# Seven block products from tile 8 of phase 0, their results in a stream of their own, and the RWKV jobs' state chain in two PSUM banks

## The chip, the cores and the metric

The kernel runs on one core of a Trainium2 chip. The metric is device time in microseconds (us) for one execution. Three runs of the kernel before gave 2259.75, 2262.86 and 2265.27 us; the median is 2262.86 us. A difference of about 0.2% (4.5 us) is what a measurement of this kernel can tell from none.

## The reference

One decoder layer is applied to a prompt of 1024 tokens and to eight single-token samples. Everything is float32; the model width is 1024 and the hidden width of the FFN 2816.

```python
h = x + 0.5 * rmsnorm(swiglu(rmsnorm(x, n1), gate1, up1, down1), n1_post)
proj = rmsnorm(h, n_mix) @ w_in                # 3328 columns
ya = differential attention (4 heads)          # of the first 1536 columns
yb = rwkv7_time_mix (8 heads of 64)            # of the other 1792
h = h + rmsnorm(concat(ya, yb) @ w_out, n_mix_post)
h = h + 0.5 * rmsnorm(swiglu(rmsnorm(h, n2), gate2, up2, down2), n2_post)

# rwkv7: per head and token, a state s (64 x 64)
sa = s @ (-kk_t)
s  = s * w_t + outer(sa, kk_t * a_t) + outer(v_t, k_t);   y_t = s @ r_t
```

It returns the layer's output, the keys and values, and the last states.

## The kernel before, in words

**Phases and halves.** The tokens are cut in two halves of 512 (one of them with the eight sample columns, 520). The first FFN is phase 0 (half 0) and phase 1 (half 1), the second FFN phase 2 and phase 3. Between them each half goes through the projection (stream `proj`), the RWKV part (streams `job0`, `job1`), attention (`attn0`, `attn1`), the output projection (`out` for half 0, `outb` for half 1). The FFN of one half fills TensorE while the mixing of the other half runs: phase 1 lies beside the mixing of half 0, phase 2 beside that of half 1. Phases 0 and 3 have no such neighbour.

**FFN.** `s_trunk` (L1034) goes over the 22 tiles of 128 hidden columns. A product in float32 accuracy is three matmuls in fp32r, with weights and data split into a high and a low part (`mm3`, L698). A plain tile takes gate and up for two column chunks of 256 or 264: 4 x 24 matmuls. In phases 0 and 3, from the tile that `FAST` names (L35), two tiles at a time are made with Strassen-like products instead (`seven`, L1098): the two tiles and the two column halves form a 2 x 2 block problem, and gate and up take 7 x 12 matmuls of 260 columns each in place of 8 x 12. `s_combine` (L994) makes the sums of the data blocks first and signals `combined`; `sums` (L940) makes the sums of the weight blocks. After each product VectorE adds it out of PSUM to the buffers v, and when a block is whole, `gates` (tanh and product) or `ups` (product, split into two parts) is applied to it; `late` and `was` hold these calls back by one product. `down` (L1160) then multiplies a finished group of tiles with the down weights and adds each result to the y tile (`trunk_xl0` in the profile's and the order's names) on VectorE. It runs behind the gate and up of the next group. The groups are in `GROUPS` (L102): for `FAST` 10, phase 0 has [0,1,2], [3,4], [5,6,7], [8,9] and then pairs; for `FAST` 8, [0,1,2], [3,4], [5], [6,7] and then pairs.

**Jobs.** `job` (L1680) is one pair of heads over 512 tokens in chunks of 64; four jobs in each half, two sets of buffers (job 0 and 2 are label `job0`, job 1 and 3 are `job1`). The front (mixing, norms; bank `dec`, and `cb` beside it) runs under the lock `front`, one job at a time. Then a job takes its set's lock and the bank `aux0` or `aux1`, builds the products of a chunk's rows (masked, `L`), transposes U (`pa`), multiplies `L` with R (`pv`, bank `cb`), solves a triangular system on VectorE (31 steps, by way of DRAM), and forms Z, L and R per chunk. Last comes the chain over the eight chunks: one PSUM tile takes Z times the state `Sd` and two products of L and R that don't need the state; VectorE makes the next `Sd` from it (`scalar_tensor_tensor`, L1915), ScalarE copies the outputs. In the names of the profile the state product is `job_aux<-bset_Sd,mix_X` (or `mix_T` in half 1), the state-free ones are `job_aux<-mix_X,job_w 128x64`.

**What sets the order.** Nothing runs as written. Each generator is a stream with a queue for each engine; every operation is recorded through one helper (so the profile shows L325 for all) and a list scheduler (`run`, L484) picks the next operation by an estimate of when it could start and how late it may be. Within one stream an engine's operations keep the order in which they were recorded; between streams only data, PSUM slots and locks count. A PSUM bank is handed from tile to tile in the order of recording. A stream may record up to 80 operations ahead (`AHEAD`, L91). The plan is made eight times and the best one by its own estimate is built, so a change in one place moves rows everywhere.

## Time and profile before

| | |
|---|---|
| median of three runs | 2262.86 us |
| the profiled execution | 2261.48 us, its span 2259.7 us |
| TensorE (PE) | 2197.5 us busy, 97% |
| VectorE (DVE) | 1556.7 us, 69% |
| ScalarE (ACT) | 1072.1 us, 47% |
| GpSimd (POOL) | 990.4 us, 44% |

In a row of the timeline the first number is the start and the second the length, both in us; `x12` is a count of merged instructions; the bracket gives the idle time of the engine just before it and who ended that. In a row of a stretch stand, behind its length, the busy times of PE, of its weight load, DVE, ACT and POOL, then the granted TensorE clock, the share of the DMA engines and GB/s. One fp32 matmul shows as two instructions, a transpose or an fp32r matmul as one. "Busy" of a PE row is modelled, with the pipeline's latency in it.

### The profile page before, as it was taken

To read this page: it belongs to the slowest core of one execution; us is meant where nothing else is said; L and a number is where in the kernel's file an instruction comes from. 1 tells how busy PE (TensorE), PEld (TensorE's weight loads), DVE (VectorE), ACT (ScalarE), POOL (GpSimd) and SP (SyncE) were. 2 spreads that over 40 slices of the span, in tenths; PEclk is the share of its full clock that TensorE was granted. 3 is DMA by queue.
4 is the path that set the end of the run, shared out by engine and by line. 5 is a ranking of instruction groups with operands and counts; after the bars stand their busy time and mean duration, and the time that the engine had idled before them with its cause. 6 is when DMAs were issued, how large, how long until landed. Compare 5 with 4: busy or idle time off the path is not lost. (4 is left out here: it accounts for less than half of the span.)

```text
span 2259.7 us, 42127 instructions
## 1 busy us (share of the span) xinstructions
PE 2197.5 (97%) x15575; PEld 1963.4 (87%) x15575; DVE 1556.7 (69%) x3577; ACT 1072.1 (47%) x2214; POOL 990.4 (44%) x818
## 2 busy tenths in 40 slices
PE   8999999999999999999999999999999999999998
PEld 8999998898877678987877777778888989999998
DVE  7757888656677667559585666786774366777776
ACT  6524444544453257444353445435664555444444
POOL 3525555533332573455353432345443355444443
PEclk9999999999999999999999999999999999999999
DMA  7322233445333574655464444486436848333433
GB/s 257 113 94 90 89 103 125 143 145 141 95 106 105 165 231 138 223 174 158 129 205 150 134 116 144 117 238 181 122 112 191 286 126 285 130 132 107 146 140 113
DMA packets 216998, 338.83 MB, mean 150 GB/s; under 512 B 50746, under 2 KB 131930, under 8 KB 216794
## 3 DMA queue, kind: packets, MB, share of 16 engines
q1 hardware_dynamic: 216506, 335.63, 47.5%
q8 instruction: 123, 2.02, 0.4%
q14 instruction: 81, 0.66, 0.1%
q10 hardware_dynamic: 288, 0.52, 0.1%
HBM read 281.06 MB, written 55.03 MB: 149 GB/s over the span
## 5 line engine op out<-in xcount | busy, mean ns | idle before, releaser
L325 POOL TENSOR_TENSOR wts_w<-wts_raw,wts_w 128x1024 fp32r<-128x1024 f32 (+2 forms) x156 | 295.5, 1901 | 363.9 <-ACT wts_w L325 314.0
L325 PE MATMUL trunk_m<-pre_X,wts_w 128*128 128x512 f32 (+3 forms) x2352 | 428.7, 336 | 9.5 <-ACT wts_w L325 6.7
L325 PE MATMUL trunk_m<-trunk_xl,wts_w 128*128 128x256 f32 (+2 forms) x2550 | 424.1, 318 | 7.9 <-DVE trunk_xl L325 5.3
L325 PEld LDWEIGHTS trunk_m<-pre_X,wts_w 128*128 128x128 f32 x2352 | 351.6, 191 | 51.3 <-ACT wts_w L325 5.6
L325 PEld LDWEIGHTS trunk_m<-trunk_xl,wts_w 128*128 128x128 f32 x2550 | 358.7, 189 | 40.1 <-DVE trunk_xl L325 7.0
L325 PE MATMUL trunk_m<-pre_T,wts_w 128*128 128x512 f32 (+3 forms) x2016 | 386.0, 343 | 3.3 <-DMA wts_w<-Lg 1.3
L325 PEld LDWEIGHTS trunk_m<-pre_T,wts_w 128*128 128x128 f32 x2016 | 307.6, 188 | 45.5 <-issue 4.8
L325 ACT CAST wts_w<-wts_raw 128x1024 fp32r<-128x1024 f32 (+3 forms) x299 | 244.5, 833 | 193.3 <-PE trunk_m L325 133.0
L325 PE MATMUL proj_m<-tail_xl,lin_w 128*128 128x256 f32 (+2 forms) x1920 | 322.4, 323 | 1.1 <-DVE init_E L325 0.7
L325 PEld LDWEIGHTS proj_m<-tail_xl,lin_w 128*128 128x128 f32 x1920 | 271.6, 189 | 36.1 <-issue 9.8
L325 DVE TENSOR_TENSOR trunk_xl<-trunk_xl,trunk_m 128x264 f32<-128x264 f32 (+2 forms) x343 | 165.1, 493 | 55.3 <-PE trunk_m L325 53.6
L325 POOL TENSOR_TENSOR lin_w<-lin_raw,lin_w 128x1024 fp32r<-128x1024 f32 x42 | 101.4, 2414 | 204.9 <-ACT lin_w L325 191.1
L325 POOL TENSOR_TENSOR trunk_xl<-trunk_t,trunk_xl 128x512 fp32r<-128x512 f32 (+3 forms) x81 | 88.4, 1092 | 179.4 <-ACT trunk_xl L325 179.1
L325 DVE TENSOR_TENSOR wts_w<-wts_raw,wts_w 128x1024 fp32r<-128x1024 f32 (+3 forms) x113 | 114.5, 1018 | 20.6 <-ACT wts_w L325 19.2
L325 ACT CAST lin_w<-lin_raw 128x1024 fp32r<-128x1024 f32 x52 | 54.5, 1049 | 94.1 <-PE proj_m L325 74.2
L325 ACT CAST wts_w<-wts_lraw 128x512 fp32r<-128x512 f32 x94 | 55.7, 619 | 67.4 <-DMA wts_lraw<-in_ffn_down_dram 28.3
L325 PE MATMUL trunk_aux<-trunk_xl,wts_w 128*128 128x264 f32 (+1 forms) x570 | 78.7, 284 | 0.0
L325 POOL TENSOR_TENSOR wts_w<-wts_lraw,wts_w 128x512 fp32r<-128x512 f32 x41 | 57.3, 1399 | 41.7 <-ACT wts_w L325 38.5
L325 PEld LDWEIGHTS trunk_aux<-trunk_xl,wts_w 128*128 128x128 f32 x570 | 72.6, 189 | 0.3 <-DVE trunk_hres L325 0.2
L325 ACT CAST wts_w<-wts_dec 128x512 fp32r<-128x512 f32 x30 | 17.6, 587 | 108.4 <-DVE wts_dec L325 108.4
L325 ACT CAST trunk_xl<-trunk_t 128x512 fp32r<-128x512 f32 (+3 forms) x96 | 46.3, 483 | 47.1 <-DVE trunk_t L325 45.3
L325 DVE TENSOR_TENSOR trunk_t<-trunk_g,trunk_m 128x512 f32<-128x512 f32 (+2 forms) x71 | 40.8, 576 | 35.9 <-PE trunk_m L325 30.7
(614 smaller groups left out, 4080.4 us busy)
## 6 DMA issues: line engine op xcount, KB each, us to landing
wts_raw<-in_ffn_gate_dram SPq DMA_DIRECT2D x87, 512.0 KB, 4.1
wts_raw<-in_ffn_up_dram SPq DMA_DIRECT2D x58, 512.0 KB, 3.6
lin_raw<-in_w_in_dram SPq DMA_DIRECT2D x52, 512.0 KB, 3.8
wts_raw<-in_ffn_down_dram SPq DMA_DIRECT2D x56, 384.0 KB, 3.4
wts_raw<-in_ffn_down_dram SPq DMA_DIRECT2D x29, 512.0 KB, 6.0
wts_w<-Ld SPq DMA_DIRECT2D x22, 512.0 KB, 3.8
mix_T<-out_dram SPq DMA_DIRECT2D x36, 256.0 KB, 3.1
Ld<-wts_w SPq DMA_DIRECT2D x24, 384.0 KB, 4.8
```

Of the source, the lines that this page charges most:

```text
L325: o = Op(eng, lambda: fn(*a, **k), st)
```

## The change

1. `FAST` of phase 0 goes from 10 to 8: tiles 8 and 9 are a pair for `seven` too, `combined` is due two tiles earlier, and the groups in front are those for 8. There is one group more, and tile 5 is a group by itself.
2. The calls of `gates` and `ups` in `seven` (phases 0 and 3) are recorded in a stream `use` of their own, not in the trunk's. On VectorE and ScalarE they need no longer come before what the trunk records after them.
3. In a job the transposes of U are 8 full 128 x 128 transposes in two groups of four with four copies, in place of 16 products of 64 x 64 with the identity and one copy.
4. The chain's tiles alternate between two banks, `aux0` and `cb` for `job0`, `aux1` and `dec` for `job1`. The state-free products come first in a tile, the state's product last.

```diff
-FAST = {0: 10, 3: 4}
+FAST = {0: 8, 3: 4}
...
-    def s_aside(self):
-        yield ("wait", "weights")
+    def s_aside(self, until="weights"):
+        yield ("wait", until)
...
+                def beside(fn, *a):
+                    was = self.cur
+                    self.cur = self.asides["trunk"]
+                    fn(*a)
+                    self.cur = was
...
                         for fn, *a in was:
-                            fn(*a)
+                            beside(fn, *a)
                         yield "pe"
                     for fn, *a in late:
-                        fn(*a)
+                        beside(fn, *a)
...
-        pa, pv = self.ps2().rearrange("p (n t) -> p n t", t=C), self.ps(bank="cb").rearrange("p (n t) -> p n t", t=C)
-        for n in range(NC):
+        pv = self.ps(bank="cb").rearrange("p (n t) -> p n t", t=C)
+        for g in range(2):
+            pa = self.ps2().rearrange("p (n w t) -> p n w t", n=4, w=2)
+            for n in range(4):
+                tr(two(pa[:, n]), two(U[:, 4 * g + n]), self.ident)
             for h, q in H:
-                mm(pa[q, n, :], U[q, n, h, :], self.ident[q, q], start=True, stop=True)
+                self.copy(U[q, 4 * g:4 * g + 4, 0, :], pa[q, :, h])
...
-        A.copy(U[:, :, 0, :], pa)
         A.copy(U[:, :, 1, :], pv)
...
         for n in range(NC):
-            pb = self.ps2().rearrange("p (n t) -> p n t", t=C)
-            mm(two(pb[:, 0:2]), two(Z[:, n]), two(Sd), start=True, stop=False)
+            pb = self.ps(bank=(f"aux{jb}", ("cb", "dec")[jb])[n % 2]).rearrange("p (n t) -> p n t", t=C)
             for h, q in H:
-                mm(pb[:, h], two(L[:, n, 2 * h:2 * h + 2]), R[:, n, h, :], start=False, stop=h == 1)
+                mm(pb[:, h], two(L[:, n, 2 * h:2 * h + 2]), R[:, n, h, :], start=h == 0, stop=False)
+            mm(two(pb[:, 0:2]), two(Z[:, n]), two(Sd), start=False, stop=True)
...
+    K.spawn(K.s_aside("trunk"), "use", (0, 3))
+    K.asides["trunk"] = K.streams[-1]
```

**First place, VectorE, the end of a pair in phase 0.** Before, the results of the second pair made by seven products (`trunk_g`, `trunk_t` with the buffers `init_rb`, `bset_sg`, `bset_la`) stand ahead of the down sums (`trunk_xl0`):

```order
L325 TENSOR_TENSOR bset_sg_30_133<-bset_la_29_132,trunk_aux0_343_2827 128x260
L325 TENSOR_TENSOR bset_la_29_132<-bset_la_29_132,trunk_aux1_344_2845 128x260
L325 TENSOR_TENSOR init_rb_10_113<-init_rb_10_113,trunk_aux1_344_2845 128x260
L325 TENSOR_TENSOR trunk_t_315_2612<-trunk_t_315_2612,bset_sg_30_133 128x260
L325 TENSOR_TENSOR init_rb_10_113<-init_rb_10_113,trunk_m0_346_2867 128x260
L325 TENSOR_TENSOR trunk_t_315_2612<-trunk_t_315_2612,bset_la_29_132 128x260
L325 TENSOR_TENSOR trunk_g_314_2611<-trunk_g_314_2611,init_rb_10_113 128x260
L325 TENSOR_TENSOR trunk_xl0_126_792<-trunk_xl0_126_792,trunk_m1_350_2894 128x256
```

Now the first down sum stands right behind the last product's sum, and the results come among the last of the sixteen down sums and behind them:

```order
L325 TENSOR_TENSOR trunk_xl0_126_796<-trunk_xl0_126_796,trunk_m0_338_2634 128x264
L325 SCALAR_TENSOR_TENSOR trunk_t_289_2245<-trunk_sq_304_2358,trunk_t_289_2245 128x260
L325 TENSOR_TENSOR trunk_xl0_126_796<-trunk_xl0_126_796,trunk_m1_339_2642 128x256
L325 TENSOR_TENSOR trunk_g_288_2244<-trunk_hres_231_1836,init_rb_10_113 128x260
L325 TENSOR_TENSOR trunk_xl0_126_796<-trunk_xl0_126_796,trunk_m2_340_2651 128x264
L325 SCALAR_TENSOR_TENSOR trunk_g_288_2244<-trunk_sq_307_2371,trunk_g_288_2244 128x260
L325 TENSOR_TENSOR trunk_g_288_2244<-trunk_g_288_2244,init_rb_10_113 128x260
L325 TENSOR_TENSOR trunk_t_289_2245<-trunk_t_289_2245,bset_sg_30_133 128x260
```

Before, three rows of results (`trunk_t` twice, `trunk_g`) stood between the sums and the first down sum; now they stand behind it, and in part behind all sixteen.

**Second place, TensorE, the chain of job 3 in half 0.** Before, a state product (`bset_Sd1`) and its state-free ones (`job1_w3`) stand together, all in the bank `aux1`, with six FFN matmuls between one step and the next:

```order
L325 MATMUL job1_aux1_1018_8905<-bset_Sd1_35_138,mix_X1_692_5440 128x128
L325 MATMUL job1_aux1_1018_8905<-mix_X1_692_5440,job1_w3_915_7821 128x64 x2
L325 MATMUL trunk_m1_1011_8820<-pre_T1_80_353,wts_w0_1005_8744 128x512
L325 MATMUL trunk_m1_1011_8820<-pre_T0_79_352,wts_w0_1005_8744 128x512 x2
L325 MATMUL trunk_m1_1011_8820<-pre_T1_80_353,wts_w0_1005_8744 128x512
L325 MATMUL trunk_m1_1011_8820<-pre_T0_79_352,wts_w0_1005_8744 128x512 x2
L325 MATMUL job1_aux1_1019_8917<-bset_Sd1_35_138,mix_X1_692_5440 128x128
L325 MATMUL job1_aux1_1019_8917<-mix_X1_692_5440,job1_w3_915_7821 128x64 x2
```

Now the banks `aux1` and `dec` take turns, the state-free products of a step stand ahead of its state product, behind the state product of the step before, and three to five FFN matmuls lie between:

```order
L325 MATMUL job1_aux1_1063_9097<-mix_X1_722_5502,job1_w3_945_7852 128x64 x2
L325 MATMUL job1_aux1_1063_9097<-bset_Sd1_35_138,mix_X1_722_5502 128x128
L325 MATMUL job1_dec_1064_9104<-mix_X1_722_5502,job1_w3_945_7852 128x64 x2
L325 MATMUL trunk_m1_1061_9064<-trunk_xl1_980_8105,wts_w1_1050_8946 128x512 x3
L325 MATMUL job1_dec_1064_9104<-bset_Sd1_35_138,mix_X1_722_5502 128x128
L325 MATMUL job1_aux1_1066_9124<-mix_X1_722_5502,job1_w3_945_7852 128x64 x2
L325 MATMUL trunk_m0_1062_9082<-trunk_xl1_980_8105,wts_w1_1050_8946 128x512 x5
L325 MATMUL job1_aux1_1066_9124<-bset_Sd1_35_138,mix_X1_722_5502 128x128
```

The steps stand closer, and the two kinds of product have changed places.

**Third place, TensorE, the chain of job 1 in half 0.** Before, its first two steps stand close together, among the transposes (`init_ident`) of job 2 and just behind the first row of job 3's front (`job1_dec` from `bset_wa`):

```order
L325 MATMUL job1_dec_872_7323<-bset_la_29_132,bset_wa_25_128 128x512
L325 MATMUL job1_aux1_891_7541<-job1_w3_778_6293,mix_X1_692_5440 64x128 x8
L325 MATMUL job0_aux0_858_7179<-init_ident_1_69,mix_X0_691_5439 64x64 x13
L325 MATMUL job1_aux1_893_7591<-bset_Sd1_35_138,mix_X1_692_5440 128x128
L325 MATMUL job1_aux1_893_7591<-mix_X1_692_5440,job1_w3_778_6293 128x64 x2
L325 MATMUL job0_aux0_858_7179<-init_ident_1_69,mix_X0_691_5439 64x64 x3
L325 MATMUL job0_cb_859_7180<-mix_X0_691_5439,job0_w2_851_7106 64x64 x8
L325 MATMUL job1_aux1_894_7598<-bset_Sd1_35_138,mix_X1_692_5440 128x128
```

Now the first step stands in the same surroundings, but the second is in `dec`, and stands behind the last product of job 3's front (`init_bones`), which has that bank:

```order
L325 MATMUL job1_dec_912_7413<-mix_T3_720_5500,init_bones_4_78 128x512
L325 MATMUL trunk_m1_956_7943<-trunk_dreg_680_5021,wts_w1_951_7925 128x512 x2
L325 MATMUL trunk_m0_957_7944<-trunk_dreg_680_5021,wts_w1_951_7925 128x512 x5
L325 MATMUL job1_dec_926_7654<-mix_X1_722_5502,job1_w3_809_6354 128x64 x2
L325 MATMUL job1_dec_926_7654<-bset_Sd1_35_138,mix_X1_722_5502 128x128
L325 MATMUL job1_aux1_928_7683<-mix_X1_722_5502,job1_w3_809_6354 128x64 x2
L325 MATMUL trunk_m0_957_7944<-trunk_dreg_680_5021,wts_w1_951_7925 128x512 x4
L325 MATMUL job1_aux1_928_7683<-bset_Sd1_35_138,mix_X1_722_5502 128x128
```

Eighty-four rows of TensorE's order lie between the first step's state product and the second's, where three lay between them before. In half 1 job 1's chain is parted in the same way.

More of the change, by code (lines that the diff above doesn't have):

```diff
@@ L1224, in s_trunk @@
             yield from down(len(groups) - 1, True)
+        self.signal("trunk")
     def s_stats(self, ph):
```

## Prediction

> **What bounds the kernel now.** I read the page's first line and its busy times first, then the stretches of 50 us, then TensorE's timeline where a stretch is not full.
>
> ```profile
> span 2259.7 us, 42127 instructions
> PE 2197.5 (97%) x15575; PEld 1963.4 (87%) x15575; DVE 1556.7 (69%) x3577; ACT 1072.1 (47%) x2214; POOL 990.4 (44%) x818
> 150.00:200.00 50.00, 50.00 (x419) 50.00 (x418) 34.66 (x68) 18.41 (x36) 20.26 (x16) 1.00 0.28 94
> 250.00:300.00 50.00, 50.00 (x418) 49.89 (x416) 44.97 (x92) 20.61 (x43) 26.91 (x23) 1.00 0.36 117
> 650.00:700.00 50.00, 45.13 (x376) 33.87 (x374) 33.52 (x96) 27.08 (x54) 19.00 (x13) 1.00 0.43 120
> 750.00:800.00 50.00, 45.65 (x233) 36.12 (x232) 36.20 (x78) 17.01 (x38) 30.73 (x24) 0.90 0.58 165
> ```
>
> TensorE is busy 2197.5 of 2259.7 us, so two things only can shorten the span: fewer matmuls, or less of the 62.2 us in which it stands still. The stretch at 150 (plain tiles of phase 0) and the one at 250 (pairs by seven products) are full; VectorE has 35 and 45 of 50 us there. The stretches at 650 and 750, the mixing of half 0, lack 4.9 and 4.4 us.
>
> Phase 0's own stops, from TensorE's timeline, are small and stand where a pair ends and its down products begin:
>
> ```profile
> 175.35 1.60 PE L325 MATMUL trunk_aux<-pre_X,wts_w 128*128 128x260 f32 x12
> 176.79 1.60 PE L325 MATMUL trunk_m<-pre_X,wts_w 128*128 128x260 f32 x12
> 178.23 1.61 PE L325 MATMUL trunk_m<-comb_dreg,wts_w 128*128 128x260 f32 x12
> 232.02 2.41 PE L325 MATMUL trunk_m<-trunk_xl,wts_w 128*128 128x256 f32 x18 [0.33 <-DVE trunk_xl L325]
> 322.15 1.72 PE L325 MATMUL trunk_m<-pre_X,wts_w 128*128 128x260 f32 x12 [0.38 <-ACT trunk_hres L325]
> 329.23 2.41 PE L325 MATMUL trunk_m<-trunk_xl,wts_w 128*128 128x256 f32 x18 [0.55 <-DVE trunk_xl L325]
> 361.03 3.45 PE L325 MATMUL trunk_m<-trunk_xl,wts_w 128*128 128x264 f32 x24 [0.60 <-DVE bset_la L325]
> ```
>
> One step of a job's state chain, from the timelines of TensorE, VectorE and ScalarE, and all state products grouped by form with the idle time ahead of them:
>
> ```profile
> 632.07 0.49 PE L325 MATMUL job_aux<-bset_Sd,mix_X 128*128 128x128 f32 x2 [0.27 <-ACT mix_X L325]
> 632.39 0.56 PE L325 MATMUL job_aux<-mix_X,job_w 128*128 128x64 f32 x4
> 632.99 0.35 DVE L325 SCALAR_TENSOR_TENSOR bset_Sd<-job_aux,job_ec,init_bones 128x128 f32<-128x128 f32 x1 [1.43 <-PE job_aux L325]
> 633.37 0.42 ACT L325 COPY mix_X<-job_aux 64x64 f32<-64x64 f32 x2 [0.88 <-DVE bset_Sd L325]
> 633.85 0.49 PE L325 MATMUL job_aux<-bset_Sd,mix_X 128*128 128x128 f32 x2
> L325 PE MATMUL job_aux<-bset_Sd,mix_X 128*128 128x128 f32 x64 | 13.9, 301 | 2.7 <-ACT mix_X L325 1.6 <-DVE mix_X L325 0.8
> L325 PE MATMUL job_aux<-bset_Sd,mix_T 128*128 128x128 f32 x64 | 13.1, 286 | 2.9 <-ACT mix_T L325 1.6 <-DVE mix_T L325 1.3
> ```
>
> A step takes 633.85 - 632.07 = 1.78 us at its shortest, and its last member is the ScalarE copy that frees the bank, not the new state (done at 633.34). TensorE stood still 2.7 + 2.9 = 5.6 us ahead of state products, of it 1.6 + 1.6 = 3.2 us for that copy and 0.8 + 1.3 for VectorE's sum that makes Z, which the change leaves.
>
> **The change, part by part.** The sum is made against the profiled execution, 2261.48 us (span 2259.7 and 1.8 around it); it lies 1.4 us below the median of 2262.86, and the forecast is moved by that.
>
> *Tiles 8 and 9 by seven products.* A pair costs 8 x 24 = 192 matmuls plain and 14 x 12 = 168 by seven. Twelve of 260 columns take 176.79 - 175.35 = 1.44 us, 0.12 each; the 24 that go are worth 2.9 us, and in a full stretch all of it shows: **-2.9**. The block sums must be ready two tiles earlier. Their last row before is this one, and the first product that needs them starts at 178.23, 57 us later, of which two plain tiles (192 x 0.12 = 23 us) and the down products of two (2 x 48 x 0.12 = 12 us) move away:
>
> ```profile
> 120.54 0.42 DVE L325 TENSOR_TENSOR comb_T<-comb_sq,comb_T 128x260 fp32r<-128x260 f32 x1
> 198.44 1.09 DVE L325 TENSOR_TENSOR trunk_xl<-trunk_xl,trunk_m 128x256 f32<-128x256 f32 x3
> ```
>
> So that wait stays covered by some 20 us. The pair's weight sums and 14 more adds on VectorE lie where it had 35 of 50 us and will have some 45, as at 250, where TensorE is full: nothing. Were that cover gone, TensorE would run at VectorE's pace there, at most a few us. *Tile 5 as a group by itself* adds sixteen down sums, each behind three matmuls only: 16 x 3 x 0.12 = 5.8 us of TensorE against sixteen sums that come every (1.09 - 0.42) / 2 = 0.34 us when three stand together (5.4 us), and take up to 0.43 one by one (6.9 us). Between 0 and 1.1 us of waiting; I take **+0.5**.
>
> *Results in a stream of their own.* At a pair's end the down sums no longer queue behind the results on VectorE. The waits that this can take are 0.33, 0.38 and 0.55; the 0.60 before the last down of the phase is nearly the same thing, but the results are then wanted at once by the last group. Between 0 and 1.9 us; I take **-1.3**. What is late next are the results themselves, and they are wanted only one group later. In phase 3 nothing waits at those places, so nothing is gained there.
>
> *Transposes of U.* Rows of TensorE's timeline for the old form and for full transposes as the kernel already makes them of another tile (BK), with the stretches around the latter (the clock is the third number from the right):
>
> ```profile
> 629.24 0.97 PE L325 MATMUL job_aux<-init_ident,mix_X 64*64 64x64 f32 x26
> 1368.23 1.09 PE L325 MATMUL job_aux<-init_ident,mix_T 128*128 128x128 f32 x8 [0.60 <-ACT job_w L325]
> 1360.00:1370.00 10.00, 8.69 (x70) 6.29 (x69) 1.56 (x3) 7.72 (x16) 0.44 (x1) 1.00 0.30 85
> 1370.00:1380.00 10.00, 9.84 (x158) 7.66 (x160) 5.43 (x10) 5.74 (x15) 1.37 (x1) 1.00 0.54 146
> 1266.27 2.87 DMA Md<-job_w
> 1270.51 5.69 DMA job_LT<-Md
> ```
>
> Sixteen old products are 32 instructions, 32 x 0.97 / 26 = 1.2 us; eight full ones take 1.1 us. Over eight jobs that is between -0.8 and 0; I take 0. The second four now wait for the first copies, about 1 us a job; that lies beside the solve's way through DRAM (2.9 + 5.7 us in the chain of waits, the last two rows). The copies add four short rows to engines that are busy 69% and 47%.
>
> *The chain.* Work on TensorE stays the same. The copy leaves the step, since the next step writes the other bank: the 3.2 us go, **-3.2**. The bounds are 0 and -5.6. What is late next is the state itself: product, `scalar_tensor_tensor` (0.35 us) and the next product, about 1.1 us a step by these rows, less than the 1.78 now. The state-free products stand behind the state product of the step before; if ScalarE is late with the copies of the bank they write, TensorE stops there.
>
> Sum: -2.9 + 0.5 - 1.3 - 3.2 = -6.9, so 2254.6 for this execution and 2256.0 beside the median. The planner's new order elsewhere I take at nothing; of the 62.2 us in which TensorE stands still, any part in the mixing stretches may fall otherwise, by some us to either side.
>
> Here a rule can be weighed. The copy's wait of 1.6 us for each form is the row. The Trainium skill, in "TensorE: Matmul & The Clock Gate", section "HAM oscillation — how this bites in real kernels", reports of a matmul kernel that a second PSUM buffer "gave no further gain (125.5 us)" beside 126.6. By that the chain's term would be about 0 instead of -3.2.
>
> **The rivals.** *Only the matmuls count (about 2260).* The copy's waits come back under another name, as do the pair ends: 2262.9 - 2.9 + 0.5 = 2260.5. For it: the waits are small and scattered, and each new order makes its own. Against it: both named queues are really gone from the order.
>
> *The chain is parted (about 2270, slower).* This is the third place in the order. Job 1's second step waits in `dec` for the whole front of job 3, set 1 is released later, and job 3 with the attention behind it starts later.
>
> ```profile
> 641.59 0.34 DVE L325 SCALAR_TENSOR_TENSOR bset_Sd<-job_aux,job_ec,init_bones 128x128 f32<-128x128 f32 x1
> 655.54 1.10 PE L325 MATMUL job_dec<-mix_T,init_bones 128*128 128x512 f32 x2 [1.02 <-DVE job_st L325]
> 770.00:780.00 10.00, 6.50 (x25) 4.28 (x24) 8.20 (x16) 2.39 (x6) 6.40 (x5) 0.76 0.40 119
> 780.00:790.00 10.00, 9.94 (x39) 8.43 (x40) 7.06 (x17) 2.50 (x6) 1.83 (x1) 0.73 0.48 133
> 1865.30 1.49 DVE L325 SCALAR_TENSOR_TENSOR pre_T<-pre_sq,init_cols,pre_T 128x256 fp32r<-128x256 f32 x1
> 1892.67 5.78 PE L325 MATMUL trunk_m<-pre_T,wts_w 128*128 128x264 f32 x46 [1.31 <-DMA wts_w<-Lg]
> ```
>
> Before, job 1's last state was made at 641.59. Now seven steps begin after 655.54 + 1.1; at 1.1 to 1.78 us each they end at 664 to 669, so set 1 comes 22 to 27 us late, and so in half 1. TensorE has FFN matmuls to put in, and the data of phase 3 were ready at 1866.8, 26 us before phase 3 began. The rival decides where half of the 22 us in one half finds no FFN work beside it: +11, without the chain's gain: 2256.0 + 3.2 + 11 = 2270. Against it: that is the very thing the planner plans around.
>
> *More than the copy goes (about 2251).* After the stops at 773 the clock is 0.76 and 0.73 for 10 us each, (0.24 + 0.27) x 10 = 5.1 us of matmuls lost. A chain without that stop may keep the clock: 2256.0 - 5.1 = 2250.9.
>
> *Transposes let the clock fall (about 2263).* The eight transposes at 1368 ran with the clock at 1.00. If in each of eight jobs they and as much work behind them ran at half clock, 8 x 0.94 = 7.5 us would be lost: 2263.5. By this the Trainium skill, same page, section "Part 4: PE-mode transpose", speaks against the change: a transpose "doesn't count as PE-busy the same way" for the clock. The trace doesn't agree: the two stretches show 1.00.
>
> **How the numbers follow.** Forecast 0.48, only the matmuls 0.20, parted chain 0.21, more than the copy 0.08, transposes 0.03. Faster by over 0.2% means below 2258.3: the third rival and 0.42 of the forecast, 0.50 in sum. Within 0.2% (to 2267.4) are the first rival, the fourth and the other 0.06 of the forecast: 0.29. Slower is the parted chain, 0.21. 0.2% is about what a measurement here can tell from no change. The forecast's own bounds are -2.9 - 1.9 - 5.6 - 0.8 = -11.2 and -2.9 + 1.1 = -1.8, so 2251.7 to 2261.1; to hold 8 in 10 the range reaches down past the third rival's middle to 2248 and up to the parted chain's 2270.
>
> **What would show it.** Right: 216 instructions fewer on PE (24, and 32 - 8 in each of eight jobs), stretches of phase 0 full and phase 1 beginning 3 to 4 us earlier; no wait of a state product for ScalarE; steps of about 1.2 us. The second term is wrong if rows at pair ends still wait for VectorE, the third if the down products of tile 5 do. The parted chain shows as a gap of over 20 us between the first and second `Sd` of job 1, and decides if TensorE idles behind it or if phase 3 begins with a wait for its data. The forecast is wrong if the idle time of TensorE, 62.2 us now, does not fall by some 4 us.

## The result, and the profile after

| | before | after |
|---|---|---|
| median (six runs each) | 2261.32 us | 2248.24 us |
| range of the runs | 2257.60 to 2265.27 | 2241.64 to 2250.67 |
| profiled execution, span | 2261.48, 2259.7 us | 2241.64, 2239.8 us |

The ratio is 0.994, with a 95% interval of 0.9924 to 0.9956: 13.1 us between the medians and 13.6 by the ratio, where 6.9 were forecast. The profiled execution of the changed kernel is the fastest of its six, 6.6 us below their median; a difference of the two traces holds these 6.6 us as well.

The first line and the busy times of the page after:

```profile
span 2239.8 us, 41775 instructions
PE 2191.0 (98%) x15359; PEld 1955.6 (87%) x15359; DVE 1543.8 (69%) x3596; ACT 1094.0 (49%) x2258; POOL 1023.7 (46%) x845
```

PE has 15575 - 15359 = 216 instructions fewer, as counted. It stands still for 2239.8 - 2191.0 = 48.8 us, 13.4 less than before. The stretches after, and the long stretch from the first matmul of phase 1 to the first of phase 3 (columns as in the prediction; the first two numbers are the length and PE's busy time):

```profile
150.00:200.00 50.00, 50.00 (x419) 50.00 (x418) 41.60 (x87) 21.46 (x43) 27.52 (x21) 1.00 0.36 116
250.00:300.00 50.00, 50.00 (x419) 50.00 (x418) 45.76 (x95) 20.89 (x44) 28.02 (x22) 1.00 0.36 116
380.00:1869.50 1489.50, 1460.04 (x9339) 1229.19 (x9340) 966.87 (x2335) 744.40 (x1540) 663.59 (x510) 1.00 0.52 158
650.00:700.00 50.00, 49.83 (x402) 38.91 (x402) 26.66 (x78) 28.71 (x68) 16.84 (x13) 1.00 0.40 114
750.00:800.00 50.00, 46.44 (x244) 37.12 (x241) 31.82 (x64) 13.62 (x32) 35.30 (x27) 0.93 0.63 188
```

The same long stretch of the kernel before:

```profile
384.00:1887.00 1503.00, 1461.90 (x9528) 1232.75 (x9528) 985.98 (x2350) 726.62 (x1506) 648.84 (x497) 0.99 0.52 156
```

Phase 0 is 4 us shorter (phase 1 begins at 380.0 in place of 384.1). The long stretch, which I call the middle, is 13.5 us shorter, and most of that is PE's idle time: 1503.00 - 1461.90 = 41.1 us before, 29.5 after. Phase 3 is 2.4 us shorter. Phase 0 from PE's timeline after: tile 4's and tile 5's down products, the first product that needs the block sums, a pair's end, and the end of the phase:

```profile
100.23 11.64 PE L325 MATMUL trunk_m<-trunk_xl,wts_w 128*128 128x256 f32 x96
123.58 6.31 PE L325 MATMUL trunk_m<-trunk_xl,wts_w 128*128 128x256 f32 x48
144.10 1.61 PE L325 MATMUL trunk_aux<-comb_dreg,wts_w 128*128 128x260 f32 x12
319.75 0.87 PE L325 MATMUL trunk_aux<-trunk_xl,wts_w 128*128 128x256 f32 x6
369.18 1.71 PE L325 MATMUL trunk_m<-trunk_xl,wts_w 128*128 128x256 f32 x12 [1.14 <-DVE trunk_xl L325]
371.30 1.00 PE L325 MATMUL trunk_m<-trunk_xl,wts_w 128*128 128x264 f32 x6 [0.40 <-DVE trunk_xl L325]
```

From its start to the start of the next row (129.73) tile 5's group takes 6.15 us, 0.128 for each of its 48 matmuls; the group of two takes 111.70 - 100.23 = 11.47 us, 0.119 for each of 96. That is 0.4 us, close to the 0.5 that was put down. The block sums are not waited for. No row between the pairs has a bracket any more; the waits have gone to the phase's last group, where the results of the last pair are wanted at once. Six rows there wait 3.05 us in all (1.14, 0.40, 0.30, 0.30, 0.32, 0.59), where four rows of the kernel before waited 2.1. So PE's idle time in the whole of phase 0 fell by 0.4 us only, from 10.65 to 10.23; the rest of the 4 us is busy time, 373.4 to 369.8.

The chain after, first unbroken in job 0 of half 0 (PE), then the groups of state products with their idle time:

```profile
567.21 0.44 PE L325 MATMUL job_aux<-bset_Sd,mix_X 128*128 128x128 f32 x2
567.49 0.56 PE L325 MATMUL job_cb<-mix_X,job_w 128*128 128x64 f32 x4
568.67 0.38 PE L325 MATMUL job_cb<-bset_Sd,mix_X 128*128 128x128 f32 x2
568.89 0.56 PE L325 MATMUL job_aux<-mix_X,job_w 128*128 128x64 f32 x4
570.07 0.38 PE L325 MATMUL job_aux<-bset_Sd,mix_X 128*128 128x128 f32 x2
...
576.86 0.38 PE L325 MATMUL job_cb<-bset_Sd,mix_X 128*128 128x128 f32 x2
L325 PE MATMUL job_aux<-bset_Sd,mix_X 128*128 128x128 f32 x32 | 6.8, 294 | 0.0
L325 PE MATMUL job_aux<-bset_Sd,mix_T 128*128 128x128 f32 x32 | 6.4, 281 | 0.0
L325 PE MATMUL job_dec<-bset_Sd,mix_X 128*128 128x128 f32 x16 | 3.9, 333 | 2.4 <-DVE bset_Sd L325 2.4
```

Seven steps take 576.86 - 567.21 = 9.65 us, 1.38 each, where the shortest took 1.78 before. No state product waits for ScalarE; of 5.6 us of idle time ahead of them 2.4 are left, in one place. And the second chain of half 0 is parted, as the second rival said: its first state product starts at 620.47, its second in `dec` at 645.32, behind another job's front (`init_bones`):

```profile
620.47 0.44 PE L325 MATMUL job_aux<-bset_Sd,mix_X 128*128 128x128 f32 x2
642.46 1.02 PE L325 MATMUL job_dec<-mix_T,init_bones 128*128 128x512 f32 x2
645.32 0.44 PE L325 MATMUL job_dec<-bset_Sd,mix_X 128*128 128x128 f32 x2
```

PE has FFN matmuls in between. Phase 3 begins with this row:

```profile
1869.52 2.68 PE L325 MATMUL trunk_m<-pre_T,wts_w 128*128 128x264 f32 x20 [1.90 <-DVE trunk_xl L325]
```

It waits 1.9 us for a row of VectorE; before, there was a wait of 1.31 us for weights a few rows later (1892.67). The last row that makes its data (`pre_T`) ends at 1853.3 us, 16 us earlier, so nothing there is late by the 22 to 27 us of the rival. So the local forecasts came true, most of them, and yet the gain is twice the sum. The rows that shrank most beside the forecast ones are waits of jobs and of attention of which the change says nothing; smaller waits grew elsewhere. From the waits of PE, before (columns: in all, times, longest):

```profile
PE job_aux L325 <- DVE job_hres L325: 7.0, 7, 2.7
PE job_aux L325 <- DVE mix_X L325: 4.4, 4, 2.0
PE attn_m L325 <- ACT mix_w L325: 3.0, 2, 2.7
```

After, the third has no row left, and the others are:

```profile
PE job_aux L325 <- DVE job_hres L325: 0.6, 2, 0.4
PE job_aux L325 <- DVE mix_X L325: 0.5, 1, 0.5
```

### The profile page after: what moved, and what is told of

It is laid out like the page before. It is cut to its first block, busy times and chain, and to the rows that moved or that the text cites. A ratio compares the mean times of both kernels' runs of the same rounds, so it can differ in the third digit from the quotient of the medians.

```text
span 2239.8 us, 41775 instructions
## 1 busy us (share of the span) xinstructions
PE 2191.0 (98%) x15359; PEld 1955.6 (87%) x15359; DVE 1543.8 (69%) x3596; ACT 1094.0 (49%) x2258; POOL 1023.7 (46%) x845
## 5 line engine op out<-in xcount | busy, mean ns | idle before, releaser
L325 POOL TENSOR_TENSOR wts_w<-wts_raw,wts_w 128x512 fp32r<-128x512 f32 (+2 forms) x164 | 305.1, 1864 | 331.0 <-ACT wts_w L325 289.2
L325 PE MATMUL trunk_m<-pre_X,wts_w 128*128 128x512 f32 (+3 forms) x2040 | 391.5, 344 | 7.8 <-ACT wts_w L325 5.4
L325 PE MATMUL trunk_m<-pre_T,wts_w 128*128 128x512 f32 (+3 forms) x1800 | 362.3, 351 | 3.6 <-DVE trunk_xl L325 2.3
L325 ACT CAST wts_w<-wts_raw 128x512 fp32r<-128x512 f32 (+3 forms) x299 | 242.5, 827 | 237.7 <-PE trunk_m L325 130.8
L325 PEld LDWEIGHTS trunk_m<-pre_X,wts_w 128*128 128x128 f32 x2040 | 311.2, 190 | 49.1 <-ACT wts_w L325 5.9
L325 PEld LDWEIGHTS trunk_m<-pre_T,wts_w 128*128 128x128 f32 x1800 | 282.1, 189 | 45.0 <-issue 2.6
L325 DVE TENSOR_TENSOR trunk_xl<-trunk_xl,trunk_m 128x256 f32<-128x256 f32 (+2 forms) x362 | 171.8, 489 | 59.5 <-PE trunk_m L325 59.0
L325 PE MATMUL trunk_m<-comb_T,wts_w 128*128 128x260 f32 x660 | 84.6, 283 | 0.0
L325 PEld LDWEIGHTS trunk_m<-comb_T,wts_w 128*128 128x128 f32 x660 | 81.7, 188 | 0.0
L325 PE MATMUL trunk_aux<-trunk_xl,wts_w 128*128 128x256 f32 (+1 forms) x546 | 75.1, 282 | 0.0
```

Source lines behind the costliest of these rows:

```text
L325: o = Op(eng, lambda: fn(*a, **k), st)
```

## The experiments

**Two theories.** *M*: the gain is made of the four parts, each by its own mechanism, and the chain was sized too small. *R*: the list scheduler makes a new order out of any edit; how the jobs then fall among the FFN's matmuls is a draw worth several us, and the order of the kernel before was a bad one. "us against before" below is (ratio - 1) x 2260, against runs of before in the same session.

**One part alone.** Four kernels: before with `FAST` at 8 (one_fast), with the stream of results (one_use), the full transposes (one_tr), the two-bank chain (one_chain). The lines are those of the change; for one_fast and one_chain:

```diff
-FAST = {0: 10, 3: 4}
+FAST = {0: 8, 3: 4}
```

```diff
-            pb = self.ps2().rearrange("p (n t) -> p n t", t=C)
-            mm(two(pb[:, 0:2]), two(Z[:, n]), two(Sd), start=True, stop=False)
+            pb = self.ps(bank=(f"aux{jb}", ("cb", "dec")[jb])[n % 2]).rearrange("p (n t) -> p n t", t=C)
             for h, q in H:
-                mm(pb[:, h], two(L[:, n, 2 * h:2 * h + 2]), R[:, n, h, :], start=False, stop=h == 1)
+                mm(pb[:, h], two(L[:, n, 2 * h:2 * h + 2]), R[:, n, h, :], start=h == 0, stop=False)
+            mm(two(pb[:, 0:2]), two(Z[:, n]), two(Sd), start=False, stop=True)
```

and for one_use and one_tr:

```diff
                         for fn, *a in was:
-                            fn(*a)
+                            beside(fn, *a)
```

```diff
+            for n in range(4):
+                tr(two(pa[:, n]), two(U[:, 4 * g + n]), self.ident)
             for h, q in H:
-                mm(pa[q, n, :], U[q, n, h, :], self.ident[q, q], start=True, stop=True)
+                self.copy(U[q, 4 * g:4 * g + 4, 0, :], pa[q, :, h])
```

> The kernel before with the seven block products from tile 8 and nothing else of the change. Theory M (the gain is made of the parts, each by its own mechanism): 24 matmuls x 0.12 us = 2.9 us less, tile 5's group by itself up to 1.1 us dearer, so 1.8 to 2.9 us faster than before. Theory R (most of the gain is the planner's new order, a draw that any edit of the stream would make anew): anything from 8 us faster to 8 us slower, with the difference spread over the mixing of the halves and not in phase 0, whose first product of phase 1 comes 2 to 3 us earlier by both.

> The kernel before with the pairs' results in a stream of their own and nothing else of the change. Theory M: the three waits at pair ends in phase 0 (0.33, 0.38, 0.55 us) go, 0 to 1.9 us faster, and phase 1 begins about 1 us earlier. Theory R: several us to either side, in the mixing of the halves.

> The kernel before with the full transposes of U in two halves and nothing else of the change. Theory M: 0 to 0.8 us faster, not told from no change. Theory R: several us to either side. A third case, that the earlier copies of U shorten each job's front: jobs' waits on VectorE and ScalarE fall by some us of the 23 that they sum to, and the time with them.

> The kernel before with the state chain in two banks, state-free products first, and nothing else of the change. Theory M in the size that the changed kernel's trace suggests (a chain of 10 to 12 us in place of 15 to 20 takes other waits of the jobs along, of the kind of 7.0 us in which products of a job waited for VectorE's job_hres): 6 to 10 us faster. The prediction's own size: 3 us faster. The rival that parting the chain costs: slower, by up to 11 us, and hidden in the changed kernel by another part. Theory R: several us to either side, with the jobs' waits (23 us in sum before) not below 18.

Measured: ratios 0.992 (0.9904 to 0.9935), 0.9995 (0.998 to 1.001), 0.9963 (0.9947 to 0.9979) and 1.0022 (1.0012 to 1.0033), so -18.1, -1.1, -8.4 and +5.0 us. They sum to -22.6, the four together gave -13.6. `FAST` alone beats the whole change, the transposes gave more than ten times their bound, and the chain, the biggest term of the forecast, makes the kernel slower. Only one_use lies where M puts it. R was too narrow as well: it gave one_fast 8 us to either side. Two side forecasts can be read from the waits of PE. In one_tr the waits of job products for VectorE and ScalarE fell from 21.9 to 9.1 us, as the third case of its text says. But in plac_b below they are 10.5 us with no edit at all, so this does not tell the third case from a new order. In one_chain they are 13.8 us, under the 18 that R set there, in a kernel that is slower than before: the jobs' waits alone don't set the time.

**Other orders of the same work.** The planner has two constants that change no operation, only choices between near-equal candidates. PE keeps its 15575 instructions; of the others a few move to another engine (VectorE 3577 before, 3583 and 3578 in the two kernels).

```diff
-SLACK = 0.02
+SLACK = 0.025
```

```diff
-HOLD = 0.6
+HOLD = 0.55
```

> The kernel before with the planner's tie margin SLACK 0.025 in place of 0.02 and nothing else: the same instructions of the same sizes, of which the planner puts some 1,070 of TensorE's 14,194 matmuls elsewhere. Theory M (the time follows the parts' own work and waits): within 2 us of before. Theory R (an order of the jobs among the FFN's matmuls is worth several us to either side, whatever the edit that shakes it): 4 us or more from before, to either side, with the difference in TensorE's idle time and in the time lost to a lower granted clock between the first matmul of phase 1 and the first of phase 3.

> The kernel before with the planner's constant HOLD 0.55 in place of 0.6 and nothing else: the same instructions, some 1,020 of TensorE's matmuls in other places. Theory M: within 2 us of before. Theory R: 4 us or more from before, to either side, and not by the same amount as with the other constant.

> The changed kernel with the planner's margin SLACK 0.025 and nothing else. If the changed kernel's 13 us are made of 6.9 us of parts and some 6 of a luckier order than that of before, other orders of the same work lie 10 to 16 us below before, to either side of the changed kernel by 2 to 4 us. If the parts alone are worth the 13 us: within 1 us of the changed kernel. If the changed kernel's order were the lucky one: slower than it by 4 us or more.

> The changed kernel with the planner's constant HOLD 0.55 and nothing else. As for the other constant: 10 to 16 us below before if orders scatter by 2 to 4 us, within 1 us of the changed kernel if they don't matter here, slower by 4 us or more if its order was the lucky one.

Measured for before: 0.9969 (0.9956 to 0.9982) and 0.9976 (0.9963 to 0.9988), -7.0 and -5.4 us with no change of work: R. For the changed kernel: 0.9935 (0.992 to 0.9951) and 0.9952 (0.9937 to 0.9967), -14.7 and -10.8, so its own order (-13.6) is neither lucky nor unlucky among these three. Under the same constants on both sides the change is worth -13.6, -14.7 + 7.0 = -7.7 and -10.8 + 5.4 = -5.4 us; the mean is -8.9. The intervals make each of the three uncertain by some 4 us, so the -6.9 of the local sum is not excluded as the worth of the change between equal settings.

**The chain, with the order held.** Putting the state-free products first in the one old bank (chain_order) makes the planner keep its order: by its plan none of the FFN's matmuls moves against the jobs' rows.

```diff
-            mm(two(pb[:, 0:2]), two(Z[:, n]), two(Sd), start=True, stop=False)
             for h, q in H:
-                mm(pb[:, h], two(L[:, n, 2 * h:2 * h + 2]), R[:, n, h, :], start=False, stop=h == 1)
+                mm(pb[:, h], two(L[:, n, 2 * h:2 * h + 2]), R[:, n, h, :], start=h == 0, stop=False)
+            mm(two(pb[:, 0:2]), two(Z[:, n]), two(Sd), start=False, stop=True)
```

For both halves of the edit (pin_chain) the kernel plans with the old chain, notes the rank of each operation, and then puts the new chain's operations out by those ranks:

```diff
+PLAN = {'fast': 0, 'tr': 0, 'chain': 0}
+EMIT = {'fast': 0, 'tr': 0, 'chain': 1}
...
+            if best is not None and self.pin:
+                heads = (st.q[e][0] for st in self.streams for e in ENGINES if st.q[e] and not st.q[e][0].left)
+                o = min(heads, key=lambda o: self.pin[0].get(o.key, 1e9))
```

> The kernel before with the state-free products ahead of the state product in each step of the chain, still in one bank. The planner leaves the FFN's matmuls where they were (not one of them moves against the jobs' rows), so this is the one part that can be seen without a new order. Theory M: the copy's wait of 3.2 us stays and only moves from the state product to the state-free one, so within 1 us of before. Theory R: the same, within 1 us, since the order is kept; a difference of 4 us or more would speak against it.

> The kernel before with the chain of the change (two banks, state-free products first), but with the order that the planner makes for the old chain kept: each instruction is put out at the place that its counterpart has in the kernel before, as far as the new banks allow (433 of 11,157 matmuls from phase 1 on stand elsewhere, 128 of them by the edit itself, and 111 FFN matmuls; in one_chain it is 1,314 and 625). Theory M with the prediction's size: 3.2 us faster than before. Theory R, by which one_chain's 5 us of loss came from its order: faster than before by 0 to 5 us. The rival that two banks cost by themselves (the chain waits in the banks of other streams): slower than before by 3 us or more, as one_chain was.

chain_order: 0.9992 (0.9981 to 1.0003), no difference, as both theories said. pin_chain: 1.1131 (1.1108 to 1.1154), 2515.91 us, 256 us slower. Job 1's chain of half 0, once it has the bank `dec`, is faster than in any kernel shown so far; state and state-free products from PE's timeline, 0.94 us a step (L338 is the same helper line, in a longer file). Job 0's chain there, with FFN matmuls fixed between its steps, still takes some 2.2 us a step.

```profile
654.73 0.49 PE L338 MATMUL job_aux<-bset_Sd,mix_X 128*128 128x128 f32 x2
655.18 0.66 PE L338 MATMUL job_dec<-mix_X,job_w 128*128 128x64 f32 x4
655.67 0.47 PE L338 MATMUL job_dec<-bset_Sd,mix_X 128*128 128x128 f32 x2
656.12 0.66 PE L338 MATMUL job_aux<-mix_X,job_w 128*128 128x64 f32 x4
656.61 0.47 PE L338 MATMUL job_aux<-bset_Sd,mix_X 128*128 128x128 f32 x2
```

The middle of this kernel, two stretches of 10 us in it, and four of its longest waits:

```profile
383.70:2143.80 1760.10, 1545.72 (x9527) 1284.14 (x9528) 989.73 (x2351) 727.61 (x1504) 636.03 (x496) 0.93 0.44 134
960.00:970.00 10.00, 5.67 (x20) 4.23 (x20) 7.00 (x16) 4.34 (x14) 3.04 (x2) 0.50 0.00 1
...
980.00:990.00 10.00, 2.83 (x10) 2.15 (x10) 4.69 (x23) 1.68 (x3) 1.58 (x2) 0.50 0.43 150
PE trunk_m L338 <- ACT wts_w L338: 24.9, 8, 6.0
PE job_aux L338 <- DVE job_hres L338: 16.3, 8, 5.5
...
PE prep_cb L338 <- DMA bset_la<-out_dram: 15.2, 1, 15.2
PE attn_m L338 <- DVE mix_w L338: 14.9, 2, 11.6
```

PE stands still 1760.10 - 1545.72 = 214.4 us in the middle and runs at a granted clock of 0.93 there, 0.50 where it has little to do. The waits are not the chain's: weights (`wts_w`), the solve's rows (`job_hres`), attention (`mix_w`) and transfers stand in each engine's fixed row, as I read it behind jobs that have come too late. Of what was expected only the sign of one rival came (two banks cost by themselves), at eighty times its size: the edit needs a new order, and what that order is worth is part of the edit. Up to the parting the kernel keeps pace with before: job 1's first state product starts at 630.58 us (630.28 before), the second at 653.84 (632.07 before), and the loss grows behind that. Whether the parting alone or the other 305 rows that had to move did it isn't told apart by this run, and no run put out the old chain by such ranks to price the method itself.

**Is it one of the parts after all?** one_fast's 18.1 us asked for a theory F: the block products bring more than their matmuls.

> The kernel before with the seven block products from tile 8 and, beside it, the planner's margin SLACK 0.025. Two kernels that differ from before in such a constant alone ran 7.0 and 6.1 us faster than it. Theory R (the order is a draw; the seven block products themselves are worth 1.8 to 2.9 us): 2 to 3 us faster than the kernel with that margin alone, so about 9 us faster than before, and not the 18.4 us of one_fast. Theory F (the seven block products bring more than their matmuls, say because the shorter phase 0 lets everything behind it start earlier against the transfers): 15 to 20 us faster than before again.

> The changed kernel with the old chain (one bank, state product first) and the other three parts. Theory M, with the term of the prediction: 3.2 us slower than the changed kernel. The reading of one_chain (5.2 us slower than before by itself) as a cost that the chain always brings: 5 us faster than the changed kernel, which would make it the fastest of these kernels. Theory R: to either side of the changed kernel by some us.

fast_p1 (`FAST` at 8 and `SLACK` 0.025): 0.9905 (0.9888 to 0.9921), -21.5, for F; R had said about 9. no_chain (the change with the old chain): 0.9978 (0.9967 to 0.999), -5.0, so the same block products with two more parts lost most of it. That asked for a second order of each and for the parts that might take it back:

> The kernel before with the seven block products from tile 8 and the planner's constant HOLD 0.55, a third order of that work. The two orders so far ran 18.4 and 21.7 us faster than before; two other orders of the old work ran 7.0 and 6.1 us faster. Theory F (the seven block products are worth some 15 us, of which only 2.4 are matmuls): 15 to 22 us faster than before. Theory R (orders scatter, and two good ones were drawn): anywhere between 3 and 20 us faster, with the middle of the range, 9 us, the likeliest.

> The kernel before with two parts, the seven block products from tile 8 and the full transposes of U. The changed kernel without its chain, which is these two and the stream of results, lost 14 us against the block products alone. Theory U (the stream of results costs some 10 us where the block products are in): 16 to 25 us faster than before. Theory T (the transposes cost it): 3 to 8 us faster. Theory R: anywhere between 3 and 20 us faster.

> The changed kernel without the stream of results, so the block products, the transposes and the chain. Theory U: 5 to 10 us faster than the changed kernel, so 18 to 23 us below before. The prediction's term for the results: 1.3 us slower than the changed kernel. Theory R: to either side of the changed kernel by up to 6 us.

> The changed kernel with the old chain and the planner's margin SLACK 0.025: a second order of the work of no_chain, which was 4.9 us faster than before, where the changed kernel itself is 13 faster. If the chain is worth some 8 us beside the other parts, as the changed kernel against no_chain says: 3 to 7 us faster than before again. Theory R (no_chain's order was a bad draw): 8 to 16 us faster than before, as the orders of the changed kernel are.

> The changed kernel without the seven block products from tile 8, so the stream of results, the transposes and the chain on the old tiles. Ten kernels so far have the block products and run 4.9 to 24.9 us faster than before, 14.6 in the mean; seven that have not (before among them) run from 5 us slower to 8.4 faster, 2.8 faster in the mean. Theory F2 (in any order the block products are worth some 12 us, more than their matmuls): no faster than before by more than 5 us, so 8 us or more slower than the changed kernel. Theory R (they are worth 2.4 us and the rest is which orders were drawn): 10 us faster than before, 2 to 3 us slower than the changed kernel, give or take 6.

> The same three parts on the old tiles with the planner's margin SLACK 0.025, a second order of that work. Theory F2: again no faster than before by more than 5 us. Theory R: 10 us faster than before, give or take 6; with the kernel above the mean of the two is then 7 us or more below before.

fast_p2 is one_fast with `HOLD` 0.55; fast_tr is one_fast with the lines of one_tr; no_use is the change with `fn(*a)` put back for `beside(fn, *a)`; noch_p1 is no_chain with `SLACK` 0.025, nofast_p1 the same for no_fast, and no_fast is the change with this line:

```diff
-FAST = {0: 8, 3: 4}
+FAST = {0: 10, 3: 4}
```

All kernels, with the parts in them (F block products, U stream of results, T transposes, C chain); phase 1's start, and for the middle its length, PE's idle time in it, and the time lost to the clock (the sum over stretches of 10 us of PE's busy time x (1 - granted clock)), each from the one profiled execution, the stretches cut at the middle's two ends:

| kernel | parts | ratio, 95% interval | us against before | phase 1 at | middle | idle | clock |
|---|---|---|---|---|---|---|---|
| before | | | 0 | 384.1 | 1502.9 | 41.0 | 7.2 |
| chain_order | | 0.9992 (0.9981 to 1.0003) | -1.8 | 383.3 | 1501.0 | 38.4 | 8.3 |
| plac_b | | 0.9969 (0.9956 to 0.9982) | -7.0 | 384.5 | 1497.2 | 39.2 | 5.0 |
| plac_b2 | | 0.9976 (0.9963 to 0.9988) | -5.4 | 384.7 | 1496.5 | 38.9 | 8.1 |
| one_use | U | 0.9995 (0.998 to 1.001) | -1.1 | 378.9 | 1497.7 | 40.9 | 3.2 |
| one_tr | T | 0.9963 (0.9947 to 0.9979) | -8.4 | 384.3 | 1491.7 | 34.8 | 7.3 |
| one_chain | C | 1.0022 (1.0012 to 1.0033) | +5.0 | 383.4 | 1508.4 | 40.6 | 14.0 |
| one_fast | F | 0.992 (0.9904 to 0.9935) | -18.1 | 381.3 | 1488.2 | 34.3 | 2.5 |
| fast_p1 | F | 0.9905 (0.9888 to 0.9921) | -21.5 | 384.5 | 1476.3 | 24.4 | 2.4 |
| fast_p2 | F | 0.9963 (0.9949 to 0.9976) | -8.4 | 381.7 | 1493.5 | 40.5 | 1.7 |
| fast_tr | F T | 0.9962 (0.9947 to 0.9976) | -8.6 | 383.4 | 1485.7 | 26.7 | 4.0 |
| no_use | F T C | 0.9901 (0.9886 to 0.9916) | -22.4 | 383.1 | 1480.0 | 23.5 | 5.8 |
| no_chain | F U T | 0.9978 (0.9967 to 0.999) | -5.0 | 380.8 | 1501.8 | 40.3 | 9.0 |
| noch_p1 | F U T | 0.989 (0.9874 to 0.9906) | -24.9 | 379.0 | 1482.1 | 22.9 | 7.0 |
| no_fast | U T C | 0.9903 (0.9878 to 0.9927) | -21.9 | 381.5 | 1483.6 | 23.6 | 7.6 |
| nofast_p1 | U T C | 0.9894 (0.9868 to 0.9919) | -24.0 | 380.7 | 1489.1 | 20.7 | 13.0 |
| after | F U T C | 0.994 (0.9924 to 0.9956) | -13.6 | 380.0 | 1489.5 | 29.5 | 4.3 |
| plac_a | F U T C | 0.9935 (0.992 to 0.9951) | -14.7 | 379.9 | 1488.6 | 28.3 | 7.4 |
| plac_a2 | F U T C | 0.9952 (0.9937 to 0.9967) | -10.8 | 381.4 | 1496.2 | 30.8 | 11.2 |

F falls with no_fast and nofast_p1: without the block products the other three parts are 22 and 24 us faster than before, more than the whole change. That the stream of results costs 10 us (theory U) fits no_use at -22.4, and that the transposes cost as much (theory T) fits fast_tr at -8.6; both fall with noch_p1, which has the two parts and is the fastest of all. The same edit has either sign, by what lies around it: the chain +5.0 (one_chain), -8.6 (after against no_chain), +10.2 (plac_a against noch_p1); the block products -18.1 (one_fast) and +8.3 (after against no_fast); three parts in two orders (no_chain, noch_p1) lie 20 us apart. fast_p2, a third order of the block products, is 8.4 us faster than before, near the middle of R's range, where F had 15 to 22. Over the 19 kernels the mean is -11.2 us and the standard deviation 9; only one_chain is slower than before. That deviation has the parts in it. Among kernels with the same parts but another constant (five groups, 13 kernels) the times lie 2 to 20 us apart, a standard deviation of some 6 us within the groups. So R holds in its main point: the order alone is worth as much as the whole change. Its sizes did not hold: one_fast, fast_p1, noch_p1, no_fast and nofast_p1 are all faster than R allowed. Before is near the slow end of the 19 and the slowest of three orders of its own work. With three orders that makes a bad draw likely and does not prove it; the worth of each part may have a share in the distance.

What an order changes is seen in the table. The middle's length less its idle time and its lost clock is 1452.7 us in the mean, and between 1449.5 and 1455.7 in all 19 (before 1502.9 - 41.0 - 7.2 = 1454.7); idle time and lost clock together go from 26.8 to 54.6. The two ends, the fastest kernel and the slowest, as one row each:

```profile
379.00:1861.00 1482.00, 1459.07 (x9339) 1230.89 (x9339) 964.03 (x2341) 739.37 (x1533) 664.40 (x509) 0.99 0.52 159
```

```profile
383.40:1891.80 1508.40, 1467.85 (x9528) 1234.83 (x9528) 962.00 (x2330) 735.91 (x1516) 668.62 (x513) 0.99 0.51 156
```

noch_p1 stands still 22.9 us, one_chain 40.6, with nearly the same work on every engine. noch_p1, at 2234.43 us, beats both kernels; it is the best of 19 draws, and its only merit over no_chain is its order. Why one order idles 20 us less than another was not found: no single wait carries it, and no experiment took one order's feature into another.

## Why the prediction was wrong in size

**The failing step** is the sentence on the order: "The planner's new order elsewhere I take at nothing". A term of the size of the whole sum was put at nothing: with the work unchanged, plac_b and plac_b2 are 7.0 and 5.4 us faster than before, so any new order could gain what the forecast had for all four parts. Nothing in before's profile says so. The bounds had no term for it either: "by some us to either side" never entered 2251.7 to 2261.1, while orders of the same work scatter by some 6 us. That the measured median lies in the stated range at all is luck: it fell at the low end, which had been stretched there for another reason, the clock. Against one build of before the gain is 13.6 us, between equal settings 8.9 in the mean; how much of the 13.6 is before's order and how much the four parts stays open.

**Block products, down of tile 5, results.** In sum -3.7 was forecast for phase 0. Phase 1's start over the kernels of the table: 384.1 in the mean with neither F nor U (six), 380.2 with both (five), so -3.8; the sum holds. Its split does not: it is 380.4 with U and without F (three), 382.8 with F and without U (five), -3.7 and -1.3, which don't add up to the two together. Within a group single kernels lie up to 3 us apart, so the split is a hint only. The wait at pair ends went, as forecast. That the phase's last group wants its results at once was said, but no cost was put on it: the waits there grew by 0.9 us, which takes back most of the 1.3 us of this term, and PE's idle time in phase 0 fell by 0.4 us. Tile 5's term came close to what was worked out (0.4 for 0.5 us), and the cover of the block sums held.

**Transposes.** The four transposes at 618.90 lie in stretches of after with the clock at 1.00, so at this place the rival by which they would let it fall, and the Trainium skill's remark behind it ("TensorE: Matmul & The Clock Gate", "Part 4: PE-mode transpose"), are not borne out; what the transposes are worth by themselves is open:

```profile
618.90 0.66 PE L325 MATMUL job_aux<-init_ident,mix_X 128*128 128x128 f32 x4
610.00:620.00 10.00, 10.00 (x125) 7.53 (x123) 6.12 (x11) 5.48 (x14) 0.44 (x2) 1.00 0.49 129
620.00:630.00 10.00, 10.00 (x90) 8.92 (x89) 5.68 (x28) 4.52 (x9) 2.39 (x1) 1.00 0.34 112
```

**The chain.** Mechanism and local size were right: the copy's 3.2 us are gone and the step is shorter. That they come off the end is not shown: the kernels with and without C that differ in nothing else lie +5.0, -8.6 and +10.2 us apart. The local gain of 3.2 us drowns in that. The rule weighed there, from the Trainium skill's same page ("HAM oscillation — how this bites in real kernels"), that a second PSUM buffer brought no further gain, is so neither confirmed nor refuted for the total; the wait that the second bank takes away did go.

**The rivals.** The parted chain took place in the changed kernel and cost nothing visible: "that is the very thing the planner plans around" held. The front that holds the bank `dec` ended earlier (642.46 in place of 655.54), and the chain's last state product starts at 654.71 us. Two readings in the working of this rival were off. The row at 641.59 is not job 1's last state: two more steps follow, the last state product before is at 645.13. And phase 3 began with its first product at 1886.99, so its data were ready 20 us ahead and not 26. So the chain ended 10 us later than before, in place of 22 to 27. With the order of before it did come with a loss, of 256 us in place of the 11 that were worked out (pin_chain). The clock's rival got 7.2 - 4.3 = 2.9 of its 5.1 us, in one execution.

**What is and isn't shown.** Shown: that orders of equal work lie up to 20 us apart, that before is near the slow end of these 19 kernels, that the change came out at 5 to 14 us in three pairs of equal constants. Not shown: the worth of each part by itself, whether before's order or the parts make the gain twice the sum, and the feature that makes an order good.

## What to carry to other kernels

Where a scheduler rebuilds the whole order from any edit, one build of before and one of after compare two draws. Run each under two or three settings that change no work, and set the edit's price against that scatter, in the forecast's range as well. A local price, such as a wait that goes, can be read from the trace to 0.1 us and still say nothing of the end until the scatter is known; and a kernel that has only one build so far may have gained most from a new draw alone.

## What was unexpected of the hardware

The granted clock is a cost of the same kind as the idle time. In one_chain three stretches of half 0 show it; the last column but two is the clock:

```profile
740.00:750.00 10.00, 9.46 (x51) 6.91 (x52) 7.35 (x21) 5.03 (x9) 5.47 (x4) 0.83 0.37 108
750.00:760.00 10.00, 6.88 (x68) 4.36 (x66) 4.51 (x10) 2.39 (x4) 5.21 (x4) 0.87 0.48 166
760.00:770.00 10.00, 10.00 (x68) 7.67 (x69) 7.78 (x11) 2.05 (x4) 3.11 (x4) 0.79 0.50 159
```

Behind a stretch with 3 us of idle time (750) a full one runs at 0.79, so it loses 2 us more. But the length of a stop doesn't say whether the clock falls. In no_use a single stop of 3.42 us, which ends at 817.40, leaves the clock at 1.00; another of 3.04 us, which ends at 736.53, comes with 0.86 and 0.80:

```profile
730.00:740.00 10.00, 6.96 (x53) 4.88 (x52) 5.84 (x10) 2.85 (x6) 8.22 (x6) 0.86 0.74 211
740.00:750.00 10.00, 10.00 (x81) 7.85 (x79) 5.89 (x9) 3.33 (x6) 5.34 (x7) 0.80 0.75 209
810.00:820.00 10.00, 6.58 (x31) 5.09 (x31) 6.22 (x12) 5.16 (x13) 3.92 (x4) 1.00 0.81 231
820.00:830.00 10.00, 9.88 (x49) 7.98 (x48) 7.73 (x12) 4.12 (x13) 8.48 (x6) 1.00 0.91 266
```

And the clock can fall with no stop at all. In nofast_p1 these three stretches show PE busy throughout and lose 10.3 of that kernel's 13.0 us; small products of 8 and 32 columns stand among the FFN's there. Whether they are the cause was not tried:

```profile
720.00:730.00 10.00, 10.00 (x45) 7.66 (x43) 2.46 (x8) 2.08 (x5) 2.59 (x3) 0.79 0.61 162
730.00:740.00 10.00, 10.00 (x43) 5.99 (x43) 3.90 (x7) 1.57 (x2) 5.30 (x4) 0.50 0.64 172
740.00:750.00 10.00, 10.00 (x67) 7.54 (x67) 4.27 (x12) 3.04 (x8) 6.53 (x6) 0.68 0.53 135
```

Over the middle the lost clock was 1.7 to 14.0 us in the 19 kernels, beside 20.7 to 41.0 us of idle time.
